# Writing out VectorE's loop in a grouped softmax that streams through four buffers

## The chip, the cores and the metric

The kernel runs on one core of a Trainium2 chip. The metric is the device time of one execution in microseconds (us); lower is better. Before the change it is 1333.27 us, the median of three runs (1332.07 to 1334.61). The profile is of one execution that took 1325.78 us, with a span of 1323.5 us from its first to its last instruction.

## The reference

The input is an array of 4 x 4096 rows of 4352 float32 numbers. Each row is cut into 8 groups of 544 numbers, and a softmax is taken in each group:

```python
x_g = x.reshape(B, N, G, Dg)                       # 4, 4096, 8, 544
x_g = x_g - x_g.max(axis=-1, keepdims=True)
exp = np.exp(x_g)
out = exp / exp.sum(axis=-1, keepdims=True)
```

There are 131072 groups. Each number is read once and written once: 285.21 MB each way.

## The kernel before

**Tiling.** The groups are dealt out over the 128 partitions, 1024 to each. They are worked in 44 tiles: 41 tiles of 24 groups per partition, and at the end one each of 20, 16 and 4. A full tile holds 128 x 13056 float32, 6528 KB. There are four buffers `xt0` to `xt3`; tile t uses buffer t mod 4 (`NT` is 4), and the result is written over the input in place.

**Who does what.** Every engine has its own program, written out by hand, and they meet in semaphores.

- SyncE issues the loads. From tile 4 on it first waits until the store that used the buffer has finished (`stored`). Tile 0 comes in three loads. SyncE also issues the stores of the last two tiles.
- VectorE works in `vector_tile`, on parts of 8 groups (4 groups in the last three tiles). For each part of a tile it takes the negated maxima of the groups (line 77). Then for each part it takes the reciprocal of the sums (line 85), and multiplies the part by it (line 88).
- ScalarE works in `scalar_tile`: for every group one exponential with the maximum as bias, which also leaves the sum (line 100).
- GpSimd issues the other 42 stores, each when VectorE has finished the tile (`scaled`).

**The semaphores of VectorE.** The first reduction of a tile waits on `landed[b]`, which a load raises by 16 when it has landed. A reciprocal waits on `exp_done`, which ScalarE raises by 1 for each part. A multiplication waits on `rec_done`, which VectorE's own reciprocals raise. All these waits compare a semaphore with a constant that stands in the instruction.

**The loop.** VectorE's program is a head of four tiles, a loop of nine turns of four tiles (tiles 4 to 39), and an end of four tiles (40 to 43). As the same instructions run in each turn, the constants in them are the same in each turn, so the semaphores must be at the same values when a turn begins. For this the program turns them back: `landed[b]` by 16 after each tile (line 148), `exp_done` and `rec_done` by the parts of a turn (lines 149 and 150), and all of them once ahead of the loop (lines 141 to 144). `turn` is the number of parts in four full tiles, 12. ScalarE has a loop of its own, of ten turns (line 132), which turns back `max_done`.

The order of VectorE's work is the order of its program: three reductions, then three pairs of reciprocal and multiplication, tile after tile.

Of the kernel before, what the change touches and what calls it, by code (L numbers as in the profile page):

```python
# [1 line left out]

# [4 lines left out]


@with_exitstack
def kernel(  # L10
    ctx: ExitStack,
    tc: tile.TileContext,
    x: bass.AP,
    out: bass.AP,
):
    nc = tc.nc
    G = 8
    P = 128
    C = 8
    NT = 4  # L20
    LAST = 2
    FIRST = (8, 8, 8)
    FINE = 4
    ENDING = 3
    f32 = mybir.dt.float32
    X = mybir.AxisListType.X
    Exp = mybir.ActivationFunctionType.Exp
    xf = x.flatten_outer_dims()
    of = out.flatten_outer_dims()
    N, D = xf.shape  # L30
    Dg = D // G
    per = N * G // P
    T = 3 * G
    sizes = [T] * (per // T - 1)
    sizes += [20, 16, per - sum(sizes) - 36]
    nt = len(sizes)
    turns = (nt - 1) // NT
    start = [sum(sizes[:t]) for t in range(nt + 1)]
    assert start[nt] == per and min(sizes) > 0
    xg_all = xf.rearrange("n (g d) -> (n g) d", d=Dg)  # L40
    og_all = of.rearrange("n (g d) -> (n g) d", d=Dg)

    def dram(a, t):
        lo, hi = start[t] * P, start[t + 1] * P
        return a[lo:hi, :].rearrange("(p g) d -> p (g d)", p=P)

    def parts(t):
        size = C if t < nt - ENDING else FINE
        return [(c, min(c + size, sizes[t])) for c in range(0, sizes[t], size)]

    before = [0]
    for t in range(nt):
        before.append(before[-1] + len(parts(t)))

    landed = [tc.alloc_semaphore(f"landed{b}") for b in range(NT)]
    stored = [tc.alloc_semaphore(f"stored{b}") for b in range(NT)]
    first_landed = [tc.alloc_semaphore(f"first_landed{k}") for k in range(len(FIRST) - 1)]
    last_stored = tc.alloc_semaphore("last_stored")
    max_done = tc.alloc_semaphore("max_done")
    exp_done = tc.alloc_semaphore("exp_done")  # L60
    rec_done = tc.alloc_semaphore("rec_done")
    scaled = tc.alloc_semaphore("scaled")

    ctx.enter_context(tc.tile_critical(  # L64
        sync_engine=mybir.EngineType.Pool, no_gpsimd_drain=True))
    bufs = [ctx.enter_context(nc.sbuf_tensor(f"xt{b}", [P, T * Dg], f32)) for b in range(NT)]
    mx = ctx.enter_context(nc.sbuf_tensor("mx", [P, NT, T], f32))
    sm = ctx.enter_context(nc.sbuf_tensor("sm", [P, NT, T], f32))
    rs = ctx.enter_context(nc.sbuf_tensor("rs", [P, NT, T], f32))

    def groups(b, lo, hi):
        return bufs[b][:, lo * Dg:hi * Dg].rearrange("p (g d) -> p g d", d=Dg)

    def vector_tile(t, landed_at, done):
        b = t % NT
        for k, (lo, hi) in enumerate(parts(t)):
            i = nc.vector.reduce_max(  # L77
                out=mx[:, b, lo:hi], in_=groups(b, lo, hi), axis=X, negate=True)
            if t == 0 and k < len(FIRST) - 1:
                i.wait_op(first_landed[k], 16, "sem-ge")  # L80
            elif t == 0 or k == 0:
                i.wait_op(landed[b], landed_at, "sem-ge")
            i.then_inc(max_done, 1)
        for k, (lo, hi) in enumerate(parts(t)):
            nc.vector.reciprocal(out=rs[:, b, lo:hi], in_=sm[:, b, lo:hi]).wait_op(  # L85
                exp_done, done + k + 1, "sem-ge").then_inc(rec_done, 1)
            xg = groups(b, lo, hi)
            i = nc.vector.tensor_tensor(  # L88
                out=xg, in0=xg,
                in1=rs[:, b, lo:hi].unsqueeze(2).to_broadcast([P, hi - lo, Dg]),  # L90
                op=mybir.AluOpType.mult,
            ).wait_op(rec_done, done + k + 1, "sem-ge")
        i.then_inc(scaled, 1)

    def scalar_tile(t, done):
        b = t % NT
        for k, (lo, hi) in enumerate(parts(t)):
            xg = groups(b, lo, hi)
            for g in range(lo, hi):
                i = nc.scalar.activation(  # L100
                    out=xg[:, g - lo, :], in_=xg[:, g - lo, :], func=Exp,
                    bias=mx[:, b, g:g + 1], scale=1.0, accum_out=sm[:, b, g:g + 1])
                if g == lo:
                    i.wait_op(max_done, done + k + 1, "sem-ge")
            i.then_inc(exp_done, 1)

    def buf(t):
        return bufs[t % NT][:, :sizes[t] * Dg]

    for k, size in enumerate(FIRST):  # L110
        cols = slice(sum(FIRST[:k]) * Dg, sum(FIRST[:k + 1]) * Dg)
        nc.sync.dma_start(out=buf(0)[:, cols], in_=dram(xg_all, 0)[:, cols]).then_inc(  # L112
            first_landed[k] if k < len(FIRST) - 1 else landed[0], 16)
    for t in range(1, nt):
        if t >= NT:
            nc.sync.wait_ge(stored[t % NT], 16 * (t // NT))
        nc.sync.dma_start(out=buf(t), in_=dram(xg_all, t)).then_inc(landed[t % NT], 16)
    for t in range(nt - LAST, nt):
        nc.sync.wait_ge(scaled, t + 1)
        nc.sync.dma_start(out=dram(og_all, t), in_=buf(t)).then_inc(last_stored, 16)  # L120

    for t in range(nt - LAST):
        nc.gpsimd.wait_ge(scaled, t + 1)
        nc.gpsimd.dma_start(out=dram(og_all, t), in_=buf(t)).then_inc(stored[t % NT], 16)  # L124
    for t in range(nt - NT, nt - LAST):
        nc.gpsimd.wait_ge(stored[t % NT], 16 * (t // NT + 1))
    nc.gpsimd.drain()
    nc.gpsimd.wait_ge(last_stored, 16 * LAST)

    nc.scalar.preload_act_table(Exp)  # L130
    turn = before[NT]
    with nc.scalar.Fori(0, turns):
        for t in range(NT):
            scalar_tile(t, before[t])
        nc.scalar.sem_inc(max_done, -turn)
    for t in range(turns * NT, nt):
        scalar_tile(t, before[t] - before[turns * NT])

    for t in range(NT):
        vector_tile(t, 16, before[t])  # L140
    for b in range(NT):
        nc.vector.sem_inc(landed[b], -16)
    nc.vector.sem_inc(exp_done, -turn)
    nc.vector.sem_inc(rec_done, -turn)
    with nc.vector.Fori(1, turns):
        for t in range(NT, 2 * NT):
            vector_tile(t, 16, before[t] - turn)
            nc.vector.sem_inc(landed[t % NT], -16)
        nc.vector.sem_inc(exp_done, -turn)
        nc.vector.sem_inc(rec_done, -turn)  # L150
    for t in range(turns * NT, nt):
        vector_tile(t, 16, before[t] - before[turns * NT])


# [1 line left out]
_INS = ['x']  # L156
_OUTS = [((4, 4096, 4352), 'float32')]


# [23 lines left out]
```

## Time and profile before

| | |
|---|---|
| device time, median | 1333.27 us |
| span of the profiled run | 1323.5 us |
| VectorE busy | 1208.0 us in 399 instructions |
| one reduction, 128 x 4352 (line 77) | 4679 ns, 123 of them |
| one multiplication, 128 x 4352 (line 88) | 4692 ns, 123 of them |
| one reciprocal, 128 x 8 (line 85) | 194 ns, 123 of them |
| ScalarE busy | 755.2 us |
| one exponential of a group, 128 x 544 (line 100) | 733 ns, 1024 of them |
| a full load, from issue to landing | 46.3 us |
| a full store, from issue to landing | 48.4 us |

The profile has several views. The page gives the busy time of each engine and, in forty equal slices of the span, how far the engines and the DMA engines were busy and how many GB/s were moved. The view of waits says which engine waited for which other, how long in all, how many times, and the longest. The timeline lists instructions in order of time. The view of DMA lists the queues: `q1` carries the loads and the stores that SyncE issues, `q0` the stores of GpSimd, and `q14` the instructions that the engines fetch. Instructions that only count a semaphore, set a register or branch have no row in these views; if they take time, it can be seen only as a gap between two rows.

### The profile page before, as it was taken

How to read it: one execution, taken by the hardware profiler on the slowest of the kernel's cores; microseconds unless marked ns; L12 is line 12 of the kernel's file. 1: busy time of each engine (PE TensorE's matmuls, PEld its weight loads, DVE VectorE, ACT ScalarE, POOL GpSimd, SP SyncE). 2: the span in 40 equal slices, each digit the busy share in tenths (PEclk: the TensorE clock that was granted, in tenths of full speed). 3: DMA queues.
4: the chain of work that ended last, by engine and by line, in shares of the span. 5: the costliest groups of instructions: out<-in, count | busy, mean ns of one | idle time of the engine just before them, and what ended most of it. 6: DMA issues, size and time to landing. Idle time of an engine off the chain costs nothing.

```text
span 1323.5 us, 2707 instructions
## 1 busy us (share of the span) xinstructions
DVE 1208.0 (91%) x399; ACT 755.2 (57%) x2049; POOL 22.6 (2%) x46
## 2 busy tenths in 40 slices
DVE  7999999999998999999999999889999999999996
ACT  5556666555555556666665555555566566665553
POOL 0000000000000000000000000000000000000000
DMA  9999999999999999999999999999999999999998
GB/s 404 429 429 430 431 437 436 437 429 431 437 432 439 432 429 432 439 432 436 431 431 440 431 439 429 431 436 437 437 431 431 431 437 434 439 431 429 440 431 362
DMA packets 12964, 570.46 MB, mean 431 GB/s; under 512 B 1440, under 2 KB 1440, under 8 KB 1440
## 3 DMA queue, kind: packets, MB, share of 16 engines
q1 hardware_dynamic: 6912, 290.79, 50.9%
q0 software_dynamic: 6048, 279.64, 48.8%
q14 instruction: 4, 0.03, 0.0%
HBM read 285.21 MB, written 285.21 MB: 431 GB/s over the span
## 4 chain that ended last, share of the span: by engine, by line
DMA 72%; DVE 27%; issue 0%; ACT 0%; SPq 0%; POOLq 0%
DMA out_dram<-xt 36%; DMA xt<-in_x_dram 36%; DVE xt L88 14%; DVE mx L77 13%; DVE rs L85 0%; ACT xt L100 0%; SPq L112 0%; SPq L178 0%; POOLq L64 0%; POOLq L167 0%
## 5 line engine op out<-in xcount | busy, mean ns | idle before, releaser
L100 ACT ACTIVATE xt<-xt,mx 128x544 f32<-128x544 f32 x1024 | 749.8, 733 | 554.8 <-DVE mx L77 554.8
L77 DVE TENSOR_REDUCE mx<-xt 128x8 f32<-128x4352 f32 (+1 forms) x133 | 592.4, 4509 | 98.0 <-DMA xt<-in_x_dram 98.0
L88 DVE TENSOR_TENSOR xt<-xt,rs 128x4352 f32<-128x4352 f32 (+1 forms) x133 | 601.3, 4521 | 4.5
L100 ACT ACTIVATION_READ_ACCUMULATOR xt<-xt,mx 128x1 f32 x1024 | 191.4, 187 | 0.0
L124 POOL DMA_DIRECT2D out_dram<-xt x42 | 22.4, 534 | 1262.6 <-DVE xt L88 1262.6
L85 DVE RECIPROCAL rs<-sm 128x8 f32<-128x8 f32 (+1 forms) x133 | 25.6, 193 | 3.1 <-ACT xt L100 3.1
L130 ACT ACT_TABLE_LOAD x1 | 1.3, 1283 | 0.9 <-PEq L167 0.9
L167 POOL MEMSET const-float32-0.0<- 128x1 f32 x1 | 0.1, 98 | 0.2 <-issue 0.2
L167 POOL MEMSET const-bfloat16-1.0<- 128x1 bf16 x1 | 0.1, 101 | 0.0
L167 POOL MEMSET const-float32-1.0<- 128x1 f32 x1 | 0.1, 98 | 0.0
L167 POOL MEMSET const-uint8-127<- 128x1 uint8 x1 | 0.1, 98 | 0.0
## 6 DMA issues: line engine op xcount, KB each, us to landing
out_dram<-xt POOLq DMA_DIRECT2D x41, 6528.0 KB, 48.4
xt<-in_x_dram SPq DMA_DIRECT2D x40, 6528.0 KB, 46.3
xt<-in_x_dram SPq DMA_DIRECT2D x3, 2176.0 KB, 12.5
xt<-in_x_dram SPq DMA_DIRECT2D x1, 5440.0 KB, 43.8
out_dram<-xt POOLq DMA_DIRECT2D x1, 5440.0 KB, 24.3
xt<-in_x_dram SPq DMA_DIRECT2D x1, 4352.0 KB, 40.0
out_dram<-xt SPq DMA_DIRECT2D x1, 4352.0 KB, 14.0
xt<-in_x_dram SPq DMA_DIRECT2D x1, 1088.0 KB, 29.7
```

The lines of the kernel that those rows point to most:

```text
L77: i = nc.vector.reduce_max(out=mx[:, b, lo:hi], in_=groups(b, lo, hi), axis=X, negate=True)
L85: nc.vector.reciprocal(out=rs[:, b, lo:hi], in_=sm[:, b, lo:hi]).wait_op(exp_done, done + k + 1, "sem-ge").then_inc(rec_done, 1)
L88: i = nc.vector.tensor_tensor(out=xg, in0=xg, in1=rs[:, b, lo:hi].unsqueeze(2).to_broadcast([P, hi - lo, Dg]), op=mybir.AluOpType.mult,).w ...
L100: i = nc.scalar.activation(out=xg[:, g - lo, :], in_=xg[:, g - lo, :], func=Exp, bias=mx[:, b, g:g + 1], scale=1.0, accum_out=sm[:, b, g:g ...
L124: nc.gpsimd.dma_start(out=dram(og_all, t), in_=buf(t)).then_inc(stored[t % NT], 16)
L130: nc.scalar.preload_act_table(Exp)
L167: nc = _bacc.Bacc("TRN2", target_bir_lowering=False, num_devices=1)
```

## The change

VectorE's loop is replaced by a program in which all 44 tiles are written out. No semaphore of VectorE is turned back any more. Each wait compares with the value that the semaphore has reached by then: `landed[b]` with 16 times the number of loads that the buffer has had, and the two others with the number of parts since the start. It is meant to take the loop's own instructions and the counting back out of VectorE's stream. ScalarE keeps its loop, and the queues of loads and stores are as they were.

```diff
-    for t in range(NT):
-        vector_tile(t, 16, before[t])
-    for b in range(NT):
-        nc.vector.sem_inc(landed[b], -16)
-    nc.vector.sem_inc(exp_done, -turn)
-    nc.vector.sem_inc(rec_done, -turn)
-    with nc.vector.Fori(1, turns):
-        for t in range(NT, 2 * NT):
-            vector_tile(t, 16, before[t] - turn)
-            nc.vector.sem_inc(landed[t % NT], -16)
-        nc.vector.sem_inc(exp_done, -turn)
-        nc.vector.sem_inc(rec_done, -turn)
-    for t in range(turns * NT, nt):
-        vector_tile(t, 16, before[t] - before[turns * NT])
+    for t in range(nt):
+        vector_tile(t, 16 * (t // NT + 1), before[t])
```

## The prediction

> **What bounds the kernel now.** I read the busy shares first, then the transfer rate in slices, then the waits, and last the timeline of VectorE at the places the change touches. The shares mislead on their own: VectorE looks like the bound.
>
> ```profile
> DVE 1208.0 (91%) x399; ACT 755.2 (57%) x2049; POOL 22.6 (2%) x46
> ...
> DMA  9999999999999999999999999999999999999998
> GB/s 404 429 429 430 431 437 436 437 429 431 437 432 439 432 429 432 439 432 436 431 431 440 431 439 429 431 436 437 437 431 431 431 437 434 439 431 429 440 431 362
> DMA packets 12964, 570.46 MB, mean 431 GB/s; under 512 B 1440, under 2 KB 1440, under 8 KB 1440
> ```
>
> The line of digits says that the DMA engines have work in every slice, and the line below it that they move 429 to 440 GB/s all the way but for the first and the last slice. All of it is wanted traffic: 285.21 MB read and as much written, once each.
>
> Who waits for whom confirms it:
>
> ```profile
> POOL out_dram L124 <- DVE xt L88: 1262.6, 42, 38.1
> ACT xt L100 <- DVE mx L77: 554.8, 44, 13.5
> DVE mx L77 <- DMA xt<-in_x_dram: 98.0, 40, 8.7
> DVE rs L85 <- ACT xt L100: 3.1, 1, 3.1
> ```
>
> The columns are total, count and longest, in us. VectorE waits 98.0 us in all for loads and once for ScalarE. 8.7 us are the first load; 84.5 us are 35 waits in the stretch from 125 to 1230 us, 2.4 us for each full tile. Tile starts there lie some 30.85 us apart (for instance 1200.95 and 1231.84), and VectorE's own work on a tile is 28.30 us (66.45 less 38.15, two tiles that did not wait). So a tile brings 6528 KB in and 6528 KB out, 13.37 MB, in 30.85 us: 433 GB/s. **The transfers set the pace**, and VectorE has 2.5 us to spare in each tile. The chain of waits, with 72% DMA and 27% VectorE, only says that a buffer goes round load, compute, store; its 46.3 us per load and 48.4 us per store are stretched by sharing. By (46.3 + 48.4) / 30.85 there are three transfers under way on average.
>
> [...] 434 GB/s from 125 to 1230 us. [...] The trace before shows four fetches, 0.03 MB in all, so nearer 8 KB each[...]. The trace shows no stall at any of them.
>
> **The change, part by part.** Every one of the 399 VectorE operations stays, with the same shapes, order and partners. What goes are instructions of the sequencer. Before the loop 4 counts of `landed` and 2 of the other semaphores are turned back. In each of nine turns (tiles 4 to 39, four at a time) 4 + 2 more follow: 6 + 54 = 60 in all. With them go nine register additions, nine compare-and-branches, one branch and one register load.
>
> None has a row of its own in the profile, so I bound them. [...] The lower end is nothing. The trace decides for nothing, at the one place where the engine did not wait for data, the entry of the loop:
>
> ```profile
> 66.45 13.86 DVE L77 TENSOR_REDUCE mx<-xt 128x8 f32<-128x4352 f32 x3
> ...
> 94.74 13.86 DVE L77 TENSOR_REDUCE mx<-xt 128x8 f32<-128x4352 f32 x3
> ...
> 118.43 4.69 DVE L88 TENSOR_TENSOR xt<-xt,rs 128x4352 f32<-128x4352 f32 x1
> 123.04 13.87 DVE L77 TENSOR_REDUCE mx<-xt 128x8 f32<-128x4352 f32 x3
> ```
>
> Columns: start, duration, what ran. The row at 123.04 is tile 4, the first in the loop; six updates, a register load and a branch stand ahead of it. It starts 28.30 us after tile 3, as tile 3 starts 28.29 us after tile 2 with nothing between. It even starts 0.08 us before the modelled end of the multiplication. The control work is hidden beside a 4.69 us multiplication.
>
> At the turns of the loop the same can be read from the waits. Tiles 8, 12, 16, 20 and 24 begin a turn and waited 2.56, 2.30, 2.47, 2.43 and 2.31 us; tiles 6, 7, 9, 10 and 11, inside turns, waited 2.44, 2.39, 2.35, 2.67 and 2.83 us. A turn adds nothing. So the removal is worth 0 us on VectorE, and had it been worth something, most would go into the 2.5 us of spare time per tile: tile t's load would still land when the transfers let it. **Removed: 0 us.**
>
> What is added is length. VectorE's program grows from 138 to 410 instructions, counted in the built programs: 272 more [...] or two to three fetches of the measured 8 KB. One fetch took 1.0% of 16 engines in a 2 us window, 0.32 us on one engine. If each delays its engine and the transfer waits for its slowest engine, that is at most 3 x 0.32 = 1.0 us, and over 16 engines it is 0.06 us. I take the lower end, as many packets queue behind each other and smooth it out, and keep 1 us for the range. **Added: 0.1 us.**
>
> The waits of the new form compare with numbers that grow (16, 32, ... for `landed`, up to 133 for the other two) and wait for the same events. Behind each waiting reduction are the tile's other VectorE instructions, and ScalarE waits for their maximum; neither the order nor the moment changes. The first load, the loop of ScalarE, the queues of loads and stores and the last four tiles, already written out, stay as they are. The end after the last load has landed (1285.99 us) is 37.5 us of the same instructions: reductions, exponentials, multiplications and two stores. Sum: 1333.27 + 0.1 = 1333.3 us after rounding down.
>
> **The rivals.**
>
> First, *the control work did cost*, at turns where its price lies inside a wait that the profile gives to a load. [...] For it: a wait with several possible ends is put down to the last known one. Against it: the equal waits at turns and inside them, the free entry at 123.04[...].
>
> Second, *a fetch stalls VectorE*. In the middle it would not show. When VectorE stops as a load lands, the next load (6.7 MB), the fresh store (6.7 MB) and about half of the one before wait or move: some 16 MB, 38 us at 434 GB/s, and VectorE gains 2.5 us back per tile. Only near the end, where 410 instructions reach the tail, does a stall add in full. A mean packet is 570.46 MB / 12964 = 44 KB; at 434 / 16 = 27 GB/s per engine that is 1.6 us. A fetch behind one packet of each of the two queues waits 3.2 us and takes 0.3: 3.5 us, **slower, at 1336.8 us**. [...] Against it: four fetches before, at 28, 110, 154 and 1294 us, and no idle row beside any of them; the one at 1294 lies in the tail itself.
>
> Third, *the phases of the transfers shift* because VectorE hands over at slightly different moments. The slices vary between 429 and 440 GB/s with no trend, and the two streams hold 50.1% each. This moves the time by what runs differ anyway, 1332.07 to 1334.61, either way.
>
> **How the numbers follow.** Forecast, the transfers set the time and nothing else matters: 62%, at 1333.3. Control work did cost, wholly or half, or a favourable shift: 18%[...]. Stall or unfavourable shift: 20%, at 1336 to 1338. Within 0.2% (2.7 us) is the first; the other two give faster and slower. The range goes from 1329.0, [...] to 1337.0, which takes in one stall at the end. [...]
>
> **What would show it.** Right: VectorE's busy time stays within 1 us of 1208.0, its wait for loads near 98 us, tile starts some 30.85 us apart, 434 GB/s in the middle, and two or three more packets on the instruction queue. The forecast of no cost at the turns is wrong if waits before tiles 8, 12, 16 shrink against their neighbours' while tile starts move closer. The second rival is right if an idle row of VectorE beside an instruction packet appears, above all after 1260 us, or the last multiplication starts later than 25.2 us after the landing at 1285.99. The whole view of the bound is wrong if the transfer rate in the middle [...] falls under 430.

## The result, and the profile after

The changed kernel takes 1332.74 us (median of six runs, 1329.13 to 1334.77), the kernel before beside it 1332.66 us. The ratio is 1.0005, with a 95% interval of 0.998 to 1.003: no change that this measurement can tell. Two repetitions with 22 runs each narrowed it to 1.0017 (1.0000 to 1.0034) and 1.0018 (1.0003 to 1.0033). So the written-out program is, as far as the runs tell, a little slower, by some 2.3 us (0.0018 x 1329 us); the interval of the second repetition goes from 0.4 to 4.4 us. The ratios are estimates over all runs; the medians alone (1333.28 against 1328.84 us in the first repetition) would give 1.003, which lies inside both intervals.

The page of the changed kernel, at the lines that answer to those shown of before:

```profile
span 1330.5 us, 2628 instructions
...
DVE 1207.9 (91%) x399; ACT 755.2 (57%) x2049; POOL 22.7 (2%) x46
...
GB/s 404 424 429 435 437 433 430 435 436 430 435 435 430 433 436 435 427 435 438 432 429 438 435 429 430 441 433 430 430 443 430 430 438 435 430 432 438 434 428 288
DMA packets 12966, 570.48 MB, mean 429 GB/s; under 512 B 1440, under 2 KB 1440, under 8 KB 1440
...
q14 instruction: 6, 0.05, 0.0%
```

The last of these lines was before:

```profile
q14 instruction: 4, 0.03, 0.0%
```

The span's 2628 instructions are 79 fewer than before (2707): 60 counts, nine additions, nine compare-and-branches and one register load of VectorE's loop. VectorE has its 399 operations and is busy for the same 1208 us. The middle still moves some 434 GB/s. There are two more packets, both on the instruction queue (six against four). The last slice moves 288 GB/s instead of 362, and the DMA engines' busy share in it is six tenths instead of eight (the last digit of the page's line of DMA digits). The profiled run of before was one of the quickest of its kernel (1325.78 us) and that of after a middling one (1332.73 us), so the spans must not be compared.

The waits of the changed kernel (total, count and longest, in us):

```profile
POOL out_dram L124 <- DVE xt L88: 1269.8, 42, 38.4
ACT xt L100 <- DVE mx L77: 561.9, 44, 14.2
DVE mx L77 <- DMA xt<-in_x_dram: 105.3, 39, 9.0
```

VectorE's wait for loads went from 98.0 to 105.3 us, and the span with it. Where those 7.3 us lie is seen in VectorE's timeline, in the two places where an instruction packet passes, at 595 and at 1030 us. Columns: start, duration, what ran, and in brackets the idle time before it.

```profile
587.90 13.88 DVE L77 TENSOR_REDUCE mx<-xt 128x8 f32<-128x4352 f32 x3 [2.55 <-DMA xt<-in_x_dram]
...
619.50 13.87 DVE L77 TENSOR_REDUCE mx<-xt 128x8 f32<-128x4352 f32 x3 [3.22 <-DMA xt<-in_x_dram]
...
650.31 13.87 DVE L77 TENSOR_REDUCE mx<-xt 128x8 f32<-128x4352 f32 x3 [2.42 <-DMA xt<-in_x_dram]
...
1022.84 13.87 DVE L77 TENSOR_REDUCE mx<-xt 128x8 f32<-128x4352 f32 x3 [2.42 <-DMA xt<-in_x_dram]
...
1054.44 13.87 DVE L77 TENSOR_REDUCE mx<-xt 128x8 f32<-128x4352 f32 x3 [3.21 <-DMA xt<-in_x_dram]
...
1085.23 13.87 DVE L77 TENSOR_REDUCE mx<-xt 128x8 f32<-128x4352 f32 x3 [2.41 <-DMA xt<-in_x_dram]
```

The tile after a packet waited 3.22 and 3.21 us for its load, the next one again 2.42 and 2.41: 0.8 us each. The view of DMA, asked for the stretch from 592 to 596 us, has the packet in its last line:

```profile
q0 software_dynamic: 16, 0.84, 48.6%
q1 hardware_dynamic: 16, 0.84, 48.2%
q14 instruction: 1, 0.01, 0.7%
```

VectorE stood still for nothing but the load: it is the load that came late. In both repetitions the first tile start after each of these two packets shows the same: waits of 3.21 and 3.41 us in the first, 3.44 and 3.21 in the second, against a usual 2.4. Of the 99 other starts of tiles 6 to 40 in these three traces, four waited 3.2 us or more, so six of six is hardly chance. The two packets account for 1.6 us of the 7.3. The rest are waits of 2.7 to 3.5 us at places where no instruction packet passes (before the tiles at 338.34, 494.37 and 744.38 us, for instance). They differ from run to run and I found no cause for them; they are the scatter of this kernel.

Where the lateness comes from can be read from the sixteen marks that each transfer leaves in the trace. I read them as one from each of the sixteen DMA engines, which the trace itself does not say. Each of these tiles starts 0.02 to 0.03 us after the last of its load's marks. At the two packets the last mark falls 0.7 us further behind the second to last (from 4.40 to 5.09 us, and from 6.83 to 7.52 us). For the load that released the last full tile (tile 40), the last two marks lie 0.90 us apart before (at 1231.82 us) and 6.88 us apart after (at 1239.13 us), while without the last one the marks span 2.30 and 3.81 us. (After the 7.52 us the gap between the last two shrinks a little while the waits stay at 2.4 us: the second to last falls back, the last does not catch up.) On that reading one DMA engine is behind the others, and a tile waits for its slowest piece. The delay is not made good: from the tile at 650 us on, no full tile in the three traces of the changed kernel waited less than 2.39 us, so no shorter wait follows a late load. Why not is not shown; the page has the DMA engines busy for 90% or more in 39 of its 40 slices.

### The profile page after: what moved, and what is told of

It reads as the page before. It is cut to its first block, busy times and chain, and to the rows that moved or that the text cites. A ratio compares the mean times of both kernels' runs of the same rounds, so it can differ in the third digit from the quotient of the medians.

```text
span 1330.5 us, 2628 instructions
## 1 busy us (share of the span) xinstructions
DVE 1207.9 (91%) x399; ACT 755.2 (57%) x2049; POOL 22.7 (2%) x46
## 4 chain that ended last, share of the span: by engine, by line
DMA 65%; DVE 29%; another core or an unknown queue 5%; issue 0%; ACT 0%; SPq 0%; POOLq 0%
DMA out_dram<-xt 33%; DMA xt<-in_x_dram 32%; DVE xt L88 15%; DVE mx L77 14%; DVE rs L85 0%; ACT xt L100 0%; SPq L112 0%; SPq L117 0%; SPq L166 0%; POOLq L64 0%; POOLq L155 0%
## 5 line engine op out<-in xcount | busy, mean ns | idle before, releaser
L77 DVE TENSOR_REDUCE mx<-xt 128x8 f32<-128x4352 f32 (+1 forms) x133 | 592.4, 4509 | 105.3 <-DMA xt<-in_x_dram 105.3
```

The lines of the kernel that those rows point to most:

```text
L77: i = nc.vector.reduce_max(out=mx[:, b, lo:hi], in_=groups(b, lo, hi), axis=X, negate=True)
```

## The experiments

There were two questions: whether the loop's control work really cost nothing (theory A) or hid in the waits (B), and what a longer program costs: nothing, a fixed time of the lagging DMA engine for each fetch (A2), or a stall of the engine that fetches (C). All ratios are to the kernel before.

**The loop where VectorE is the bound.** To take the transfers out of the way, both forms were run with cut stores: the 42 of GpSimd as below, and the two of SyncE in the same way.

```diff
-        nc.gpsimd.dma_start(out=dram(og_all, t), in_=buf(t)).then_inc(stored[t % NT], 16)
+        nc.gpsimd.dma_start(out=dram(og_all, t)[:, :8 * Dg], in_=buf(t)[:, :8 * Dg]).then_inc(stored[t % NT], 16)
```

The looped one:

> The looped program, with each store cut to the first 8 groups of the tile; two thirds of the output are left out. 380 MB instead of 570 MB are moved, some 880 us at 434 GB/s, so that VectorE becomes the bound: 8.7 us to the first load, 43 tiles at 28.3 us and the end, some 1265 us. It is one half of a pair with the written-out one. Theory A (control work is hidden beside the multiplication): tile starts 28.30 us apart everywhere, at the turns of the loop too. Theory B (control work costs VectorE time): tile starts at a turn up to 0.8 us further apart (6 counts and the branch at 0.1 us), 9 turns, and 0.1 us for each tile.

The written-out one:

> The written-out program with the same cut stores, two thirds of the output left out. Theory A: the same time as the looped one with cut stores, within 1 us, tile starts 28.30 us apart. [...] Theory C (a fetch stalls VectorE): gaps of 3 us or more near the fetches, at some 43 + 128 n instructions.

They took 1229.63 us (1229.57 to 1229.76) and 1229.70 us (1229.64 to 1229.74). My estimate of 1265 us had counted the three small last tiles as full ones; the difference of the pair is what was asked. VectorE's timeline of the looped one, at tiles 7, 8 and 9:

```profile
207.90 13.87 DVE L77 TENSOR_REDUCE mx<-xt 128x8 f32<-128x4352 f32 x3
...
236.20 13.86 DVE L77 TENSOR_REDUCE mx<-xt 128x8 f32<-128x4352 f32 x3
...
264.49 13.87 DVE L77 TENSOR_REDUCE mx<-xt 128x8 f32<-128x4352 f32 x3
```

and of the written-out one:

```profile
207.95 13.87 DVE L77 TENSOR_REDUCE mx<-xt 128x8 f32<-128x4352 f32 x3
...
236.25 13.86 DVE L77 TENSOR_REDUCE mx<-xt 128x8 f32<-128x4352 f32 x3
...
264.54 13.87 DVE L77 TENSOR_REDUCE mx<-xt 128x8 f32<-128x4352 f32 x3
```

Tile 8 begins a turn of the loop: six counts, an addition and a branch stand between the two programs' rows, and both start it 28.30 us after tile 7. No row waits. A constant 0.05 us, there from tile 1 on, is all that parts them. Theory B falls where it would have to show most: at the 0.1 us for each count that is read below, the 54 counts of the nine turns alone would have made some 5 us (an estimate). Theory C falls for the written-out program, which runs straight on: it fetched at 544 and 940 us and no tile moved. The scatter went too: 0.2 us over four runs, against 8 us over the eleven runs of the kernel before beside them; here VectorE sets the time, as its waits for loads are 9.6 and 9.7 us in all, in three places before 20 us.

The trace of before says the same directly. The view of one source line does list the sequencer's instructions, which the other views leave out. Here are the first and the last that stand between tiles 3 and 4: the counts of line 142, and the register load of line 145 (shortest, median and longest duration in ns, then the start of the first and of the last in us):

```profile
L142 DVEq EVENT_SEMAPHORE  x4: 21/21/21, 118.4 to 118.7; - x4
```

```profile
L145 DVEq MOVE  x1: 36/36/36, 119.0 to 119.0; - x1
```

The multiplication ahead of them runs from 118.43 to 123.12 us. All seven instructions were begun within its first 0.6 us, about 0.1 us apart, and at each of the nine turns the branch starts 0.4 us after the last multiplication does.

**More instructions behind each tile.** An unused semaphore is counted up and down after each tile, in the written-out program.

```diff
         i.then_inc(scaled, 1)
+        for n in range(EXTRA):
+            nc.vector.sem_inc(spare, 1 if n % 2 == 0 else -1)
```

With 64:

> The written-out program with 64 more counts of an unused semaphore after each tile's last multiplication: 2816 more instructions, 180 KB, about 22 more fetches of 8 KB on VectorE's instruction stream. Theory A as in the forecast, fetches smoothed out over 16 engines and counts hidden: 1333 us, no change, VectorE busy 1208 us, its waits before a tile still some 2.5 us. Theory A2, formed from the changed kernel's trace, where the last part of a load lands 0.7 us later after each of the two fetches at 595 and 1030 us: each fetch pushes one and the same DMA engine back by 0.7 us, so 22 x 0.7 = 15 us, 1348 us, with VectorE waiting longer for loads. Theory B (counts cost VectorE time): 64 x 0.1 us is 6.4 us per tile, of which 4.7 us lie beside the multiplication and 2.5 us in the wait for the load, so no change below 0.11 us per count; at 0.2 us per count (12.8 us per tile) the tile takes 28.3 + 12.8 - 4.7 = 36.4 us and the run some 1570 us.

With 32:

> The written-out program with 32 instead of 64 counts of an unused semaphore after each tile: 1408 more instructions, 90 KB, 11 fetches more than the changed kernel. Theory A2 (each fetch of VectorE costs the lagging DMA engine a fixed time): half of what 64 counts cost, which was 1.3% over the changed kernel, so a ratio of 1.008 to the kernel before, some 1341 us. If it is the counts themselves that cost (64 took 6.4 us per tile, past the 4.7 us of the multiplication; 32 take 3.2 us and lie wholly beside it): no gap in VectorE and the ratio of the changed kernel, 1.002.

64 counts gave 1347.27 us, ratio 1.0148 (1.0124 to 1.0171); 32 gave 1339.23 us, 1.0077 (1.0052 to 1.0102). So the first form of theory A, that fetches are smoothed out, falls. A2 had the direction and the order of size: it foretold 15 us more for 64 counts, and 19.7 us were measured (16.5 to 22.7). That its 1348 us met the 1347.27 is partly luck, as the kernel before took 1328.84 us beside it and not 1333. The forecast for 32, made after the run with 64, was 1.008, and it came out. The waits of the one with 64:

```profile
DVE mx L79 <- DMA xt<-in_x_dram: 109.4, 36, 9.0
DVE mx L79 <- issue: 19.2, 10, 3.9
```

"issue" is time in which VectorE waited for nothing but its sequencer: now that 64 counts outlast a multiplication (6.3 us from the one at 242.64 us to the reduction at 248.97, against 4.69 us), they show in ten places. The one with 32 has a single such wait of 0.6 us and 13 more packets of instructions than before, and still costs 0.8%. So it is not VectorE's time for the counts. The one with 64 has 2816 more instructions than the changed kernel and 22 more packets (28 against 6), one for 128 instructions; by that the 272 instructions which the change adds are 2.1 packets (an estimate), and two came. Counts and packets grow together in this pair; the next two experiments part them.

**ScalarE written out as well.**

```diff
-    with nc.scalar.Fori(0, turns):
-        for t in range(NT):
-            scalar_tile(t, before[t])
-        nc.scalar.sem_inc(max_done, -turn)
-    for t in range(turns * NT, nt):
-        scalar_tile(t, before[t] - before[turns * NT])
+    for t in range(nt):
+        scalar_tile(t, before[t])
```

> ScalarE's loop written out as well: 859 more instructions there, [...] six or seven more fetches, and no added work on any engine. Theory A: no change against the written-out VectorE, ratio 1.000. Theory A2 (each fetch 0.7 us on one lagging DMA engine): if ScalarE's fetches fall on the engine that VectorE's do, 7 x 0.7 = 5 us more, ratio 1.004; if they fall on another, no change. Theory C (a fetch stalls its engine): gaps of some us in ScalarE's timeline at the fetches, hidden unless in the last tiles.

1337.82 us, ratio 1.0062 (1.0040 to 1.0084), with no count added. There were 13 more packets than in the changed kernel, twice what I had counted. Each exponential has a second record, the one that reads out the sum (1024 of each on the page of before). If each also counts twice in what is fetched, 2 x 859 / 128 = 13 packets follow, an estimate that fits the number. VectorE again waits for nothing but loads:

```profile
1024.07 13.87 DVE L77 TENSOR_REDUCE mx<-xt 128x8 f32<-128x4352 f32 x3 [2.43 <-DMA xt<-in_x_dram]
...
1055.64 13.87 DVE L77 TENSOR_REDUCE mx<-xt 128x8 f32<-128x4352 f32 x3 [3.19 <-DMA xt<-in_x_dram]
...
1086.43 13.87 DVE L77 TENSOR_REDUCE mx<-xt 128x8 f32<-128x4352 f32 x3 [2.41 <-DMA xt<-in_x_dram]
```

The packet at 1031.4 us is VectorE's, which the changed kernel has too, and the tile after it waits 3.19 us. The six other packets between 767 and 1190 us (at 767.5, 856.6, 943.8, 1015.6, 1100.9 and 1188.1) are those that writing out ScalarE added, and the tile after each of them waits 2.40 to 2.43 us, as usual. The marks of the loads show where these went: each time the second to last mark comes 0.5 to 0.7 us closer to the last one (from 3.85 to 3.30 us at the first of them), while VectorE's packet takes the last one 0.8 us further away. At the load that landed at 1240.35 us the two last marks lie only 1.2 us apart, and the other fourteen all lie 5.9 us or more ahead of these two. On the reading of one mark for each engine, ScalarE's packets delayed a second DMA engine, and as it was not the last, they delayed none of these six tiles. This trace is of one of the shorter of the seven runs (1333.92 us; 1330.88 to 1339.65 in all), and it does not show where the median's extra 4 to 5 us over the changed kernel lie.

**Fetches of an engine that computes nothing.** The kernel before, with VectorE's loop as it was:

```diff
         nc.sync.dma_start(out=buf(t), in_=dram(xg_all, t)).then_inc(landed[t % NT], 16)
+        for n in range(EXTRA):
+            nc.sync.sem_inc(spare, 1 if n % 2 == 0 else -1)
```

> The kernel before, VectorE looped as it was, with 64 counts of an unused semaphore after each load that SyncE issues: 2752 more instructions on an engine that computes nothing and waits some 30 us per tile, 176 KB, about 21 more fetches. Theory A2: the fetches themselves cost, whatever engine makes them: 21 x 0.8 = 17 us more, ratio 1.013. If only a fetch of VectorE costs, or its counts: ratio 1.000. If SyncE's fetches fall on a DMA engine that does not lag, less than the 17 us until it becomes the one that lags.

1353.33 us (median of five runs; a sixth, of 1366.89 us, is left out), ratio 1.0200 (1.0158 to 1.0242), more than the 17 us expected. SyncE fetches once in two tiles (at 929.9 and 992.4 us, for instance), and VectorE, whose program is that of before, waits in step with it:

```profile
905.19 13.87 DVE L79 TENSOR_REDUCE mx<-xt 128x8 f32<-128x4352 f32 x3 [2.64 <-DMA xt<-in_x_dram]
936.74 13.87 DVE L79 TENSOR_REDUCE mx<-xt 128x8 f32<-128x4352 f32 x3 [3.15 <-DMA xt<-in_x_dram]
967.74 13.87 DVE L79 TENSOR_REDUCE mx<-xt 128x8 f32<-128x4352 f32 x3 [2.62 <-DMA xt<-in_x_dram]
999.33 13.87 DVE L79 TENSOR_REDUCE mx<-xt 128x8 f32<-128x4352 f32 x3 [3.20 <-DMA xt<-in_x_dram]
1030.35 13.87 DVE L79 TENSOR_REDUCE mx<-xt 128x8 f32<-128x4352 f32 x3 [2.63 <-DMA xt<-in_x_dram]
```

Every second load is 0.5 us late. Each tile has the same 64 counts, but only every second one a packet, so this lateness is the packet's: a fetch of SyncE costs, with no change to VectorE's program at all. SyncE itself still waits 1109.7 us for stores before its loads, so its counts hold up no load. But the tiles without a packet wait 2.6 us here and 2.4 in the changed kernel. These 0.2 us for each tile stay open. To the packets themselves 22 x 0.55 = 12 us of the 26.6 can be put down, an estimate from these waits.

**The loop with turns of 300 instructions.** The same 64 counts in the looped form:

> The looped program with the same 64 counts after each tile. A turn is now 300 instructions[...]. Theory A: VectorE's spare 2.5 us per tile and some 38 us of queued transfers hide a stall at a turn; 1333 us. Theory C (a fetch after a branch stalls VectorE behind full DMA queues): a gap of 3 us or more in VectorE's timeline at each of the nine turns (before tiles 8, 12, 16, ...), and, if the following tiles cannot make it good, up to 9 x 3.5 = 30 us more. Theory A2: as many fetches as in the written-out one with 64 counts, about 20, and the same time as that, 1348 us.

1380.78 us, ratio 1.0406 (1.0383 to 1.0430): worse than the same work written out. Its waits, and two pieces of its chain around the turn of the loop at tile 8:

```profile
DVE mx L79 <- issue: 145.1, 42, 11.8
DVE mx L79 <- DMA xt<-in_x_dram: 10.0, 3, 9.0
```

```profile
250.68 9.74 issue
260.41 13.87 DVE mx L79 x3
```

VectorE now waits for its own sequencer before nearly every tile, 1.4 to 1.8 us inside a turn, and at each of the eight branches back 10.4 to 11.8 us. By its record the branch ahead of tile 8 starts at 250.61 us, right after the 64 counts and the turn's own, and the reduction it leads to at 260.41; at the seven other branches back it is 8.4 to 8.9 us. Packets of instructions begin at 253.9, 258.4 and 265.0 us, the first two of them between the branch and the reduction, and two pass there at the other branches too. The turn of the kernel before, 44 instructions, ran nine times with no packet between 154 and 1295 us. So with 300 instructions to a turn VectorE stands at each branch back while packets of instructions pass; that it stands because the start of the turn has to be fetched again is my reading of these times, not shown by itself. A turn adds 3 x 1.6 + 10.8 = 15.6 us to VectorE's work, against some 4 x 2.5 = 10 us to spare, and the chain is 73% VectorE. Theory A, that queued transfers hide it, falls for this kernel. So does A2's count: 46 more packets than before, not 20.

**The changed kernel again**, twice:

> The changed kernel once more, beside the kernel before, to narrow the interval. Theory A (the transfers set the time, the control work is hidden, and what is left is the price of three more fetches of instructions at up to 0.7 us each on the DMA engine that lags): a ratio of 1.000 to 1.002. Theory B (the control work of the loop cost something that was booked as a wait for loads): a ratio below 0.998. Theory C (a fetch stalls VectorE near the end): a ratio of 1.002 to 1.004, and a gap in VectorE's timeline after 1260 us.

> The changed kernel a third time, to narrow the interval of the smallest effect. Theory A2 (two to three more fetches at some 0.8 us each, from the runs with 32 and 64 counts): a ratio of 1.0012 to 1.002. No effect at all: 1.000, and the 1.0017 of the first repetition was scatter.

Ratios 1.0017 (1.0000 to 1.0034) and 1.0018 (1.0003 to 1.0033). The runs in which transfers set the time, by packets of instructions beyond the four of before:

| kernel | more packets | ratio | us more, (ratio - 1) x 1328.84 | for each packet |
|---|---|---|---|---|
| changed kernel, second repetition | 2 | 1.0018 | 2.4 | 1.2 |
| written out, 32 counts | 13 | 1.0077 | 10.2 | 0.79 |
| ScalarE written out too | 15 | 1.0062 | 8.2 | 0.55 |
| loop before, SyncE counts | 22 | 1.0200 | 26.6 | 1.2 |
| written out, 64 counts | 24 | 1.0148 | 19.7 | 0.82 |

The numbers of packets are read from these lines of the pages, in the order of the table:

```profile
q14 instruction: 6, 0.05, 0.0%
q14 instruction: 17, 0.14, 0.0%
q14 instruction: 19, 0.16, 0.0%
q14 instruction: 26, 0.21, 0.0%
q14 instruction: 28, 0.23, 0.0%
```

The slowdown grows with VectorE's own packets (2, 13, 24), at about 0.8 us for each. For the changed kernel itself this gives 2 x 0.8 = 1.6 us, inside its interval. The row of ScalarE is lower, and that of SyncE higher, than this price for the reasons given above, as far as they are known.

## Why the prediction was right, and where a term was off

*What bounds it.* Right: the transfers set the pace, VectorE has 2.4 to 2.5 us to spare per tile. The sharper statement is that the last of a load's sixteen marks sets it: the tiles start 0.02 to 0.03 us after it. That it is the mark of one slowest DMA engine is my reading.

*Removed: 0 us.* Right, and shown by the pair with cut stores. Two steps on the way were not. The counts and branches do have records of their own, and these show them beside the multiplication, so no bound was needed. And the equal waits at turns and inside them could not tell: a wait for a load ends when the load lands, whether or not counts run inside it. A count takes 0.1 us: in the looped kernel with 64 counts, VectorE's last multiplication of tile 8 starts at 284.11 us and the next reduction at 290.55, 6.4 us for 64 counts. The 60 counts that went are then some 6 us of VectorE's sequencer (60 x 0.1, an estimate). The six counts of a turn, 0.6 us, lie beside a multiplication of 4.69 us.

*Added: 0.1 us.* This is the term that was mis-sized. I set two or three packets at 0.32 us each on one DMA engine, and took the lower end because I assumed, with no trace behind it, that many packets smooth it out. They did not: each of the two more packets delayed the next load by 0.8 us and the delay stayed, so they cost 1.6 us by these waits, and the measured change is some 2.3 us. Even my upper end, 1.0 us, lies below the 1.6. The forecast of no change held because both are small beside 0.2%, 2.7 us; that 1332.74 us came within 1 us of 1333.3 is luck, as single runs differ by 12 us. The wait for loads did not stay near 98 us: it was 105.3, 102.2 and 101.9 us in the three traces.

*The rivals.* The first (control work did cost) fell. The second (a fetch stalls VectorE) fell for straight-line code: with cut stores, VectorE's tile starts in the written-out program stay 0.05 us behind the loop's, past both packets. In the tail, too, the last multiplication of the changed kernel starts 25.2 us after the reduction that the last awaited load releases (1318.32 less 1293.09 us), as before (1311.22 less 1285.99). At the branches back by 300 instructions VectorE does stand, and longer than I had set it: 8.4 to 9.8 us instead of 3.5, with two packets in it where I had counted one. The program before shows no such stall: its turn of 44 instructions ran with no packet between 154 and 1295 us. The third, the scatter between runs, is real: 1325.63 to 1337.62 us for the changed kernel.

## What to carry to other kernels

Where transfers set the time and the DMA engines have work all the way, ask what lands on a single one of them. In this kernel an 8 KB packet of instructions on the engine that was last, as the marks are read here, delayed the tile by 0.5 to 0.8 us, and the delay was not made good; on another engine it delayed no tile. The loop's control work was free: at the loop's entry seven instructions, begun within 0.6 us, stood beside a multiplication of 4.69 us. 64 counts, 6.4 us, were not: VectorE waited 1.4 to 1.8 us for them inside a turn. At 0.1 us each some 45 counts would fit beside the multiplication (an estimate). What the loop bought was a short program: a turn of 44 instructions ran with no packet between 154 and 1295 us. With 300 instructions to a turn it lost that, and more, with 46 more packets and 8.4 to 9.8 us at each branch back; no turn of a length between the two was measured. Judge a few microseconds in a kernel of this kind by many runs, or by waits beside one event, not by two spans.

## What was not expected of the hardware

A packet of 8 KB of instructions takes 0.31 us by most of its own records, but delays the load beside it by 0.8 us (0.5 us for SyncE's); why it costs more than its own time stays open. VectorE fetched once in 128 instructions (22 packets for 2816) and did not pause for it in straight-line code, where no tile start moved at 544 and 940 us; a branch back by 300 instructions cost 8.4 to 9.8 us each time. And the scatter of this kernel, up to 12 us, was 0.2 us as soon as transfers no longer set the time.
